# An MLP up-projection in seven block products for eight, on three token blocks for two

## The chip, the cores and the metric

One NeuronCore of one Trainium2 chip runs the whole program in one launch. The metric is the device time of one execution in microseconds (us), the median of several runs. The core has five engines with a queue each: TensorE (PE; its weight loads are shown apart as PEld), VectorE (DVE), ScalarE (ACT), GpSimd (POOL) and SyncE (SP), which here only starts DMAs. An engine works its queue in order.

## The reference, cut to what matters

One step of a one-layer streaming encoder: 2048 prompt tokens and 32 sample tokens, model width 1024. A norm, one input projection, four head groups (pooling, band attention, gated DeltaNet, GLA), and an output projection added to x give the residual x. The change touches only what follows, on 2080 tokens:

```python
h2 = _rmsnorm(x, mlp_norm_g[l])
up = jnp.square(jax.nn.relu(jnp.einsum('btd,df->btf', h2, w_up[l])))      # 1024 -> 4096
x = x + jnp.einsum('btf,fd->btd', up, w_down[l])                           # 4096 -> 1024
y = _rmsnorm(x, final_norm_g)
```

All tensors are float32. The matmuls take the type fp32r, whose values are shorter than float32; so each operand is split into a high part (a cast on ScalarE) and a low part (source minus high part, on VectorE), and each product is three matmuls: high x high, high x low, low x high.

## The kernel before

Everything is kept transposed: features lie on the 128 partitions, tokens along a row. Phase 1 (head groups and output projection) ends by storing the residual to a DRAM tensor `x2d`, feature tile by feature tile. Phase 2 is the MLP, and the change lies there.

Tokens are done in two blocks (`span`): 1024 tokens in two chunks of 512, then 1056 in three of 352. For each block, `mlp_acc` loads the residual into eight SBUF tiles `acc` (1024 features = 8 x 128), `mlp_norm` sums the squares and gets the reciprocal root into `nss` (in the profile; `self.ss` in the code), and `mlp_prep` writes the normed, scaled rows as high and low parts into `h2T`, a tile of one buffer. For block 0 this runs beside the end of the output projection: the generators are stepped between its matmuls. For block 1 the steps are taken between the output tiles of `mlp_down`, the norm from feature pair 13 on and the preparation in pair 15's turn.

The 4096 hidden features are 32 tiles of 128, taken in 16 pairs `f2`. `mlp_up(f, ...)` loads the 128 columns of w_up (1024 x 128, as a 128 x 1024 tile `wur`), splits them into two weight tiles, and for each chunk runs 8 k-tiles x 3 matmuls into one PSUM bank `u` (three buffers). Then Relu on ScalarE, max(u, 0) x relu(u) on VectorE (L1654), and the split into the tile `u`. `mlp_down` (L1658 to L1691) takes the pair before: for each chunk and each of the 8 output tiles it runs 2 x 3 matmuls into a bank `d` (three buffers), and VectorE adds the bank to `acc` (L1672). In the last pair of a block the squares of the finished `acc` are summed there (L1682 to L1687), and `final` (L1693) norms the chunk and stores it.

The order of the work: the program order above is a list of priorities. A planner in the compiler runs through it with estimated times and fixes each engine's queue, so matmuls of `mlp_up` and `mlp_down` come mixed in TensorE's queue; matmuls into one bank keep their order (`PT.order`, L96). Tiles come from pools with a fixed number of buffers taken in turn: `ld` (4) for everything loaded, `wt` (6) and `wx` (3) for weight parts, two from `wt` for one from `wx`. `wx` and the tiles `u` lie where phase 1's `hT` was and are to be had when the output projection is through. All helper matmuls are recorded under L90, all splits under L252 and L253 (L255 and L256 with a scale). Loads are started by SP, stores by ScalarE's queue.

Of the kernel before, what the change touches and what calls it, by code (L numbers as in the profile page):

```python
# [110 lines left out]
class K:  # L111
# [1417 lines left out]
    def span(self, blk):  # L1529

        return (SEQ // 2, SEQ // 2 + NS, 352, (2, 3, 4)) if blk else (0, SEQ // 2, 512, (0, 1))

    def mlp_acc(self, blk, acc):
        t0, n, _, gs = self.span(blk)
        for i in range(8):
            x = self.ac.tile([P, 1056], F32, name="acc", tag=f"acc{i}")[:, 0:n]
# [14 lines left out]
    def mlp_rows(self, blk, acc, i):  # L1551
# [3 lines left out]
        x = x[:, 0:n]  # L1555
        if acc is None:
            assert self.ready(*(("x2", g) for g in gs))
            self.nc.sync.dma_start(x, self.x2d[i][:, t0:t0 + n])
        return x, (x if acc is None else acc[i])

    def mlp_norm(self, blk, acc=None):

        nc = self.nc
        t0, n, cw, _ = self.span(blk)
        self.ss = ss = self.nm.tile([P, 1056], F32, name="nss", tag="nss")[:, 0:n]
        for i in range(8):
            x, src = self.mlp_rows(blk, acc, i)
            nc.scalar.activation(x if i else ss, src, AF.Square)  # L1568
# [3 lines left out]
        for o in range(0, n, cw):  # L1572
            self.rstd([ss[:, o:o + cw]], cw)
        yield

    def mlp_prep(self, blk, hT, acc=None):

        nc = self.nc
        n = self.span(blk)[1]
        nxt = self.mlp_rows(blk, acc, 0)  # L1580
        for i in range(8):
            x, src = nxt
            (nc.gpsimd if i % 2 or blk else nc.vector).tensor_tensor(x, src, self.ss, ALU.mult)
            self.split(hT[:, i, 0, 0:n], hT[:, i, 1, 0:n], x, self.mg[:, i:i + 1])
            if i < 7:
                nxt = self.mlp_rows(blk, acc, i + 1)
            yield

    def phase2(self):
        nc, tc, a = self.nc, self.tc, self.a  # L1590
        with ExitStack() as ctx:
# [3 lines left out]
            def wtile():  # L1595
                nwt[0] += 1
                if nwt[0] % 3:
# [3 lines left out]
            def weights(src, shape):  # L1601
                raw = self.ld.tile([P, 4 * 280], F32, name="wur", tag="ld")[:, 0:D]
                hi, lo = wtile(), wtile()
                view = (lambda x: x.rearrange("p (k f) -> p k f", k=8)) if shape else (lambda x: x)
                nc.sync.dma_start(view(raw), src)
                self.split(hi, lo, raw)
                return view(hi), view(lo)
# [5 lines left out]
            hT = self.h2.tile([P, 8, 2, 1056], F32R, name="h2T", tag="h2T")  # L1613
            with tc.tile_pool(name="wk2", bufs=1, **early) as self.wk:
# [10 lines left out]
                for z, _ in enumerate(self.fill):  # L1625
                    if self.last_part and not first:
                        first.append(weights(a["w_up"][0], True))
# [8 lines left out]
            rl = pool("rl2", 2)  # L1636
            self.wx = pool("wx", 3)
# [174 lines left out]
```

## Time and profile before

| | |
|---|---|
| median of 3 runs | 2767.6 us (2766.8 to 2770.08) |
| the profiled execution | 2760.96 us, span 2759.2 us |
| mean granted TensorE clock | 0.986 of full |
| TensorE / weight loads busy | 97% / 85% of the span |
| VectorE / ScalarE / GpSimd busy | 60% / 34% / 22% |
| first matmul of the MLP | at 1272 us of the span |
| moved by DMA | 292.88 MB, 106 GB/s in the mean |

One execution is recorded. Busy times are sums of recorded instructions; matmuls are pipelined, so one matmul's own duration (0.32 us at 352 columns) is longer than the distance to the next. The rate is read as a stretch of time over the number of matmuls in it.

### The profile page before, as it was taken

The page shows a single profiled execution, that of the slowest core. Times are in us where ns is not written, and L with a number is a line of the kernel's source. Part 1 is how long each engine was busy: PE and PEld are TensorE (multiplying, and loading weights), DVE is VectorE, ACT ScalarE, POOL GpSimd, SP SyncE. Part 2 cuts the span into 40 slices and gives each one's busy share as a digit, 9 for nine tenths or more (in the row PEclk, how much of TensorE's full clock was granted, in tenths as well). Part 3 has the DMA queues.
Part 4 walks back from the last instruction along what each step waited for, and adds up shares of the span by engine and source line. Part 5 has one row for each costly group of instructions (what it writes and reads, how often), then busy time and mean ns, then how long its engine had stood idle before and what let it go on. Part 6 is the DMA issues. An engine that isn't in the chain of part 4 may idle for free.

```text
span 2759.2 us, 41285 instructions
## 1 busy us (share of the span) xinstructions
PE 2670.6 (97%) x16044; PEld 2344.7 (85%) x16044; DVE 1652.4 (60%) x3081; ACT 933.2 (34%) x1758; POOL 620.6 (22%) x869
## 2 busy tenths in 40 slices
PE   7998998999899999989999999999999999999998
PEld 7887887888778887868888888888799999999997
DVE  6577688868876965574444445454755454545444
ACT  6535534653564343343121212131322121212122
POOL 4533554455446343230000000010300000000001
PEclk9998999999999999999999999999999999999999
DMA  5654454454546475465111112141341111111101
GB/s 173 191 158 141 135 164 142 137 162 132 167 123 175 131 224 167 131 197 170 46 46 46 54 38 61 31 124 31 112 167 54 39 54 39 54 39 48 45 31 63
DMA packets 195267, 292.88 MB, mean 106 GB/s; under 512 B 41344, under 2 KB 129680, under 8 KB 195072
## 3 DMA queue, kind: packets, MB, share of 16 engines
q1 hardware_dynamic: 123344, 231.58, 27.5%
q10 hardware_dynamic: 71664, 58.59, 6.5%
q8 instruction: 126, 2.06, 0.3%
q14 instruction: 69, 0.57, 0.1%
q0 software_dynamic: 64, 0.08, 0.0%
HBM read 227.67 MB, written 63.64 MB: 106 GB/s over the span
## 4 chain that ended last, share of the span: by engine, by line
PE 82%; DVE 9%; DMA 4%; issue 2%; ACT 2%; POOL 1%; SPq 0%; ACTq 0%; DVEq 0%; POOLq 0%
PE d L90 28%; PE u L90 26%; PE g L90 17%; PE s L90 4%; PE a L90 3%; PE l L90 2%; DVE wt L253 1%; PE s L94 1%; DVE tp L999 1%; DMA x2d<-sg 1%; DVE X L1000 1%; DVE h2T L256 1%; PE a L94 1%; DMA ldt<-w_o 1%; DVE hT L256 0%
## 5 line engine op out<-in xcount | busy, mean ns | idle before, releaser
L1672 DVE TENSOR_TENSOR acc<-acc,d 128x352 f32<-128x352 f32 (+1 forms) x616 | 360.5, 588 | 500.5 <-PE d L90 495.7
L90 PE MATMUL u<-h2T,wt 128*128 128x352 f32 (+1 forms) x2536 | 634.5, 352 | 0.0
L90 PE MATMUL d<-u,wt 128*128 128x352 f32 (+1 forms) x2576 | 624.7, 352 | 3.9 <-DVE acc L1672 3.9
L90 PE MATMUL g<-hT,wt 128*128 128x512 f32 (+2 forms) x2544 | 539.9, 361 | 15.6 <-ACT hT L252 4.7
L90 PEld LDWEIGHTS d<-u,wt 128*128 128x128 f32 x2576 | 455.5, 188 | 52.3 <-DVE acc L1672 7.0
L90 PEld LDWEIGHTS u<-h2T,wt 128*128 128x128 f32 x2536 | 451.8, 188 | 45.3 <-issue 0.5
L90 PEld LDWEIGHTS g<-hT,wt 128*128 128x128 f32 x2544 | 411.5, 192 | 80.9 <-issue 6.3
L90 PE MATMUL u<-h2T,wx 128*128 128x352 f32 (+1 forms) x1304 | 390.2, 350 | 0.0
L90 PE MATMUL d<-u,wx 128*128 128x352 f32 (+1 forms) x1264 | 356.7, 351 | 0.3 <-DVE acc L1672 0.3
L1653 ACT ACTIVATE rr<-u 128x352 f32<-128x352 f32 (+1 forms) x160 | 81.0, 515 | 635.8 <-PE u L90 594.9
L90 PEld LDWEIGHTS u<-h2T,wx 128*128 128x128 f32 x1304 | 238.9, 188 | 22.4
L90 PEld LDWEIGHTS d<-u,wx 128*128 128x128 f32 x1264 | 228.5, 188 | 22.2 <-DVE acc L1672 0.8
L90 PE MATMUL g<-wt,hT 128*128 128x256 f32 (+3 forms) x1632 | 240.8, 297 | 3.7 <-DVE sg L464 2.7
L90 PEld LDWEIGHTS g<-wt,hT 128*128 128x128 f32 (+1 forms) x1632 | 212.9, 188 | 14.6 <-issue 4.4
L253 DVE TENSOR_TENSOR wt<-ldt,wt 128x1024 fp32r<-128x1024 f32 (+1 forms) x120 | 163.2, 1360 | 65.0 <-ACT wt L252 64.4
L1687 POOL TENSOR_TENSOR fs<-fs,sq 128x352 f32<-128x352 f32 (+1 forms) x15 | 17.0, 1132 | 767.4 <-ACT sq L1685 767.4
L252 ACT CAST wt<-ldt 128x1024 fp32r<-128x1024 f32 (+1 forms) x120 | 126.0, 1050 | 114.2 <-PE g L90 66.0
L1570 POOL TENSOR_TENSOR nss<-nss,xp 128x1024 f32<-128x1024 f32 (+1 forms) x8 | 19.5, 2438 | 627.3 <-ACT xp L1568 619.4
L252 ACT CAST wt<-wur 128x1024 fp32r<-128x1024 f32 x85 | 87.7, 1045 | 185.1 <-PE u L90 101.0
L1654 DVE SCALAR_TENSOR_TENSOR rr<-u,rr 128x352 f32<-128x352 f32 (+1 forms) x160 | 92.7, 587 | 79.0 <-ACT rr L1653 78.4
L252 ACT CAST u<-rr 128x352 fp32r<-128x352 f32 (+1 forms) x160 | 82.9, 539 | 115.9 <-PE d L90 59.4
L253 DVE TENSOR_TENSOR u<-rr,u 128x352 fp32r<-128x352 f32 (+1 forms) x160 | 95.4, 617 | 23.1 <-ACT u L252 19.6
(329 smaller groups left out, 3336.1 us busy)
## 6 DMA issues: line engine op xcount, KB each, us to landing
wur<-w_up SPq DMA_DIRECT2D x64, 512.0 KB, 3.5
wur<-w_down SPq DMA_DIRECT2D x64, 512.0 KB, 3.5
ldt<-w_fm SPq DMA_DIRECT2D x56, 512.0 KB, 4.4
ldt<-w_o SPq DMA_DIRECT2D x32, 512.0 KB, 5.1
ldt<-w_tm SPq DMA_DIRECT2D x24, 512.0 KB, 4.2
fmd<-sg ACTq DMA_DIRECT2D x46, 256.0 KB, 2.8
qkr<-fmd SPq DMA_DIRECT2D x88, 128.0 KB, 3.9
xp<-x2d SPq DMA_DIRECT2D x16, 528.0 KB, 4.0
```

Source lines behind the costliest of these rows:

```text
L90: return self.order(self.k.nc.tensor.matmul(out, lhsT, rhs, start=not have, stop=True, skip_group_check=True))
L94: return self.order(self.k.nc.tensor.transpose(out, src, self.k.c["ident"][:n, :n]))
L252: nc.scalar.copy(hi, src)
L253: (eng or nc.vector).tensor_tensor(lo, src, hi.bitcast(F32), ALU.subtract)
L256: nc.vector.scalar_tensor_tensor(lo, src, scale, hi.bitcast(F32), ALU.mult, ALU.subtract)
L999: v.tensor_tensor(tv, bc(B[:, w:32, q:w], [P, r, w]), bc(X[:, q:w, 0:w], [P, r, w]), ALU.mult)
L1000: v.tensor_tensor(X[:, w:32, 0:w], X[:, w:32, 0:w], tv, ALU.subtract)
L1570: (nc.gpsimd if i % 2 else nc.vector).tensor_tensor(ss, ss, x, ALU.add)
L1653: nc.scalar.activation(rr[:, :cw], ps.t[:, :cw], AF.Relu)
L1654: nc.vector.scalar_tensor_tensor(rr[:, :cw], ps.t[:, :cw], 0.0, rr[:, :cw], ALU.max, ALU.mult)
L1672: nc.vector.tensor_tensor(x, x, ps.t[:, :cw], ALU.add)
L1687: (nc.vector if i % 2 else nc.gpsimd).tensor_tensor(fs[i % 2], fs[i % 2], sq, ALU.add)
```

## The change

Three token blocks of 696, 696 and 688 tokens, each of two equal chunks of h = 348 or 344, replace the two. `mlp_up` takes a pair of feature tiles at once. With A the pair's weights in 2 x 2 blocks (feature tile x half of the 1024 inputs) and B the block's input in 2 x 2 blocks (half of the inputs x half of the tokens), it forms seven products of sums (Strassen's method in Winograd's form) where the plain way has eight. `mlp_prep` writes seven input combinations of h columns each, `h2T` being 4 x 2 x 7 x 348, and `up_weights` builds the weight sums on GpSimd. Products are added up in PSUM where they can be; three are copied out or summed on the way. The bank `u` becomes three banks of one buffer each, u1, u2 and u4, and u1 takes four products in turn. Square and Relu are laid out anew: Relu on ScalarE, the square on GpSimd, over 696 tokens at once.

Weight parts come in turn from `wt` and `wx`, which has 6 buffers now; a pair uses 11 (A 2, s2/s4 2, s1 1, s3/A22 2, w_down 4). In the last pair of every block `mlp_down` takes the last two pairs together (in the kernel before only in the last block).

```diff
     def span(self, blk):
-        return (SEQ // 2, SEQ // 2 + NS, 352, (2, 3, 4)) if blk else (0, SEQ // 2, 512, (0, 1))
+        return ((0, 696, 348, (0, 1)), (696, 696, 348, (1, 2)), (1392, 688, 344, (2, 3, 4)))[blk]
...
+    COMB = {n: z for z, n in enumerate(("B11", "T3", "T1", "B21", "B22", "T2", "T4"))}
     def mlp_prep(self, blk, hT, acc=None):
-            (nc.gpsimd if i % 2 or blk else nc.vector).tensor_tensor(x, src, self.ss, ALU.mult)
-            self.split(hT[:, i, 0, 0:n], hT[:, i, 1, 0:n], x, self.mg[:, i:i + 1])
+        for k in range(4):
+            xa, sa = self.mlp_rows(blk, acc, k)
+            xb, sb = self.mlp_rows(blk, acc, k + 4)
+            nc.vector.scalar_tensor_tensor(xa[:, 0:n], sa, self.mg[:, k:k + 1], self.ss, ALU.mult, ALU.mult)
+            nc.scalar.mul(xb[:, 0:n], sb, self.mg[:, k + 4:k + 5])
+            nc.gpsimd.tensor_tensor(xa[:, n:n + h], xa[:, 0:h], xa[:, h:n], ALU.subtract)
+            nc.gpsimd.tensor_tensor(xb[:, 0:n], xb[:, 0:n], self.ss, ALU.mult)
+            yield
+            nc.gpsimd.tensor_tensor(xa[:, h:n], xb[:, h:n], xa[:, h:n], ALU.subtract)
+            nc.vector.scalar_tensor_tensor(xb[:, n:n + h], xa[:, n:n + h], -1.0, xb[:, h:n], ALU.mult, ALU.subtract)
+            self.split(hT[:, k, 0, 0:3 * h], hT[:, k, 1, 0:3 * h], xa[:, 0:3 * h])
+            yield
+            nc.vector.scalar_tensor_tensor(xa[:, 0:h], xb[:, n:n + h], -1.0, xb[:, 0:h], ALU.mult, ALU.subtract)
+            self.split(hT[:, k, 0, 3 * h:6 * h], hT[:, k, 1, 3 * h:6 * h], xb[:, 0:3 * h])
+            yield
+            self.split(hT[:, k, 0, 6 * h:7 * h], hT[:, k, 1, 6 * h:7 * h], xa[:, 0:h])
             yield
...
-                if nwt[0] % 3:
+                if nwt[0] < 3 or nwt[0] % 2:
                     return self.wtile()[:, 0:D]
...
+            def up_begin(f2):
+                r0, r1 = (raw(a["w_up"][2 * f2 + z].rearrange("p k f -> p (k f)")) for z in range(2))
+                return r0, r1, pair(r0)
+
+            def up_weights(r0, r1, A):
+                H = 512
+                s1 = self.nm.tile([P, H], F32, name="s1", tag="s1")
+                add = lambda o, x, y: nc.gpsimd.tensor_tensor(o, x, y, ALU.add)
+                add(s1, r1[:, 0:H], r1[:, H:D])
+                add(r1[:, 0:H], r0[:, 0:H], r1[:, 0:H])
+                add(r0[:, 0:H], s1, r0[:, 0:H])
+                add(r0[:, H:D], r0[:, 0:H], r0[:, H:D])
+                s24 = pair(r0)
+                w1 = wtile()
+                self.split(w1[:, 0:H], w1[:, H:D], s1)
+                s3a = pair(r1)
...
-            pu = pool("pu", 3, space=PSUM)
+            pu = pool("pu", 1, space=PSUM)
...
+            def mlp_up(f2, hT, h):
+                w = up_weights(*(first.pop() if first else up_begin(f2)))
...
+                def mm(z, x, y):
+                    hi, lo = w[x]
+                    o = self.COMB[y] * h
+                    for k in range(4):
...
+                        ps[z].mm(ps[z].t[:, :h], 0, P, hi[:, ks], bh)
+                        ps[z].mm(ps[z].t[:, :h], 0, P, hi[:, ks], bl)
+                        ps[z].mm(ps[z].t[:, :h], 0, P, lo[:, ks], bh)
+                def save(z, n):
+                    keep[n] = rl.tile([P, 348], F32, name="k", tag=f"k{n}")[:, :h]
+                    nc.scalar.copy(keep[n], ps[z].t[:, :h])
+                def total(z, n, o):
+                    nc.vector.tensor_tensor(o, keep[n], ps[z].t[:, :h], ALU.add)
+                def square(z):
+                    nc.gpsimd.tensor_tensor(c[z], c[z], c[z], ALU.mult)
+                    self.split(us[z][:, 0], us[z][:, 1], c[z])
+
+                mm(1, "A11", "B11")
+                save(1, 1)
+                mm(2, "A12", "B21")
+                total(2, 1, c[0][:, 0:h])
+                mm(1, "s2", "T2")
+                save(1, 2)
+                mm(4, "s1", "T1")
+                save(4, 5)
+                mm(1, "s3", "T3")
+                total(1, 5, c[1][:, h:n])
+                nc.scalar.activation(c[1][:, h:n], c[1][:, h:n], AF.Relu, scale=-1.0)
+                mm(4, "s4", "B22")
+                total(4, 2, c[0][:, h:n])
+                nc.scalar.activation(c[0], c[0], AF.Relu)
+                square(0)
+                self.tick()
+                mm(1, "A22", "T4")
+                nc.scalar.activation(c[1][:, 0:h], ps[1].t[:, :h], AF.Relu, scale=-1.0)
+                square(1)
...
-                    if blk and f2 == 15:
-                        mlp_down(us + nxt, acc, chs, t0)
+                    if f2 == 15:
+                        mlp_down(us + nxt, acc, chs, blk, side)
```

## Rows read from the trace of the kernel before

**Rows 1.** The page's first part, whole span: busy us, share, instructions of each engine.

```profile
span 2759.2 us, 41285 instructions
...
PE 2670.6 (97%) x16044; PEld 2344.7 (85%) x16044; DVE 1652.4 (60%) x3081; ACT 933.2 (34%) x1758; POOL 620.6 (22%) x869
```

**Rows 2.** The page's fourth part: shares of the chain of work by engine.

```profile
PE 82%; DVE 9%; DMA 4%; issue 2%; ACT 2%; POOL 1%; SPq 0%; ACTq 0%; DVEq 0%; POOLq 0%
```

**Rows 3.** Busy time by stretch: length, engines with instruction counts, PEclk, DMA share, GB/s.

```profile
1200.00:1272.00 72.00, 64.30 (x423) 59.70 (x422) 48.14 (x47) 27.89 (x27) 10.27 (x4) 0.93 0.65 208
...
1500.00:1700.00 200.00, 200.00 (x867) 162.37 (x866) 91.17 (x125) 34.83 (x49) 0.00 (x0) 1.00 0.15 45
1940.00:1968.00 28.00, 24.07 (x98) 17.41 (x97) 25.57 (x25) 12.35 (x13) 13.19 (x5) 1.00 0.45 144
2100.00:2300.00 200.00, 200.00 (x1241) 200.00 (x1240) 95.68 (x171) 37.59 (x66) 0.00 (x0) 1.00 0.14 43
2300.00:2600.00 300.00, 300.00 (x1863) 300.00 (x1863) 147.04 (x261) 61.07 (x106) 0.00 (x0) 1.00 0.16 48
```

**Rows 4.** Waits of TensorE's MLP, 1240 to 2759: total us, times, longest us.

```profile
PE d L90 <- DVE acc L1672: 4.1, 7, 1.5
```

**Rows 5.** Timeline, TensorE, 1249 to 1276: start, us, line, names, shapes, count.

```profile
1249.43 22.81 PE L90 MATMUL g<-hT,wt 128*128 128x288 f32 x168 [0.18 <-DVE sg L1402]
1272.08 1.08 PE L90 MATMUL u<-h2T,wt 128*128 128x512 f32 x4
```

**Rows 6.** Groups by form, 1350 to 2759: count, busy us, mean ns, idle before.

```profile
L1672 DVE TENSOR_TENSOR acc<-acc,d 128x352 f32<-128x352 f32 x360 | 185.9, 520 | 234.6 <-PE d L90 230.0 <-DMA acc<-x2d 4.2
...
L253 DVE TENSOR_TENSOR wt<-wur,wt 128x1024 fp32r<-128x1024 f32 x40 | 48.9, 1223 | 44.8 <-PE u L90 34.0 <-ACT wt L252 10.8
...
L252 ACT CAST wx<-wur 128x1024 fp32r<-128x1024 f32 x40 | 41.9, 1046 | 112.6 <-PE u L90 110.1 <-DMA wur<-w_up 2.5
...
L1653 ACT ACTIVATE rr<-u 128x352 f32<-128x352 f32 x96 | 42.8, 461 | 302.4 <-PE u L90 301.1 <-DVE u L253 0.9
...
L1583 POOL TENSOR_TENSOR xp<-xp,nss 128x1056 f32<-128x1056 f32 x8 | 22.6, 2831 | 103.3 <-DMA xp<-x2d 103.1
...
L1687 POOL TENSOR_TENSOR fs<-fs,sq 128x512 f32<-128x512 f32 x6 | 8.3, 1376 | 42.9 <-ACT sq L1685 42.9
```

**Rows 7.** Timeline of VectorE in block 1, 2309 to 2312.

```profile
2309.30 1.23 DVE L253 TENSOR_TENSOR wt<-wur,wt 128x1024 fp32r<-128x1024 f32 x1 [1.85 <-ACT wt L252]
2310.44 0.95 DVE L1672 TENSOR_TENSOR acc<-acc,d 128x352 f32<-128x352 f32 x2
```

**Rows 8.** Timeline of VectorE at the change of block.

```profile
1944.81 1.31 DVE L256 SCALAR_TENSOR_TENSOR h2T<-xp,pv,h2T 128x1056 fp32r<-128x1056 f32 x1
...
1958.44 2.32 DVE L256 SCALAR_TENSOR_TENSOR h2T<-xp,pv,h2T 128x1056 fp32r<-128x1056 f32 x1
1960.68 1.27 DVE L1672 TENSOR_TENSOR acc<-acc,d 128x512 f32<-128x512 f32 x2
1961.88 2.33 DVE L256 SCALAR_TENSOR_TENSOR h2T<-xp,pv,h2T 128x1056 fp32r<-128x1056 f32 x1
1964.12 1.21 DVE L253 TENSOR_TENSOR wx<-wur,wt 128x1024 fp32r<-128x1024 f32 x1
```

**Rows 9.** Timeline of GpSimd at the change of block.

```profile
1896.60 2.48 POOL L1583 TENSOR_TENSOR xp<-xp,nss 128x1056 f32<-128x1056 f32 x1 [59.37 <-DMA xp<-x2d]
...
1950.30 12.78 POOL L1583 TENSOR_TENSOR xp<-xp,nss 128x1056 f32<-128x1056 f32 x4 [9.77 <-DMA xp<-x2d]
```

**Rows 10.** Timeline of TensorE at the change of block, with what it waited for.

```profile
1961.41 0.95 PE L90 MATMUL d<-u,wt 128*128 128x512 f32 x3 [0.39 <-DVE acc L1672]
...
1965.99 0.96 PE L90 MATMUL d<-u,wt 128*128 128x512 f32 x3 [1.52 <-DVE acc L1672]
```

**Rows 11.** Timeline of VectorE, first addition of block 1.

```profile
2033.36 0.52 DVE L1672 TENSOR_TENSOR acc<-acc,d 128x352 f32<-128x352 f32 x1 [4.23 <-DMA acc<-x2d]
```

**Rows 12.** The page's sixth part: DMA issues, KB each, us to landing.

```profile
wur<-w_up SPq DMA_DIRECT2D x64, 512.0 KB, 3.5
```

More of the change, by code (lines that the diff above doesn't have):

```diff
@@ L1626, in phase2 @@
                     if self.last_part and not first:
-                        first.append(weights(a["w_up"][0], True))
+                        first.append(up_begin(0))
                     next(prep, None)
@@ L1635, in phase2 @@
             up = pool("up", 4)
[L1636 to L1638 removed]
+            rl = pool("rl2", 1)
+            self.wx = pool("wx", 6)
+            pu = pool("pu", 1, space=PSUM)
             pdn = pool("pdn", 3, space=PSUM)
[L1641 to L1642 removed]
+            def mlp_up(f2, hT, h):
+                w = up_weights(*(first.pop() if first else up_begin(f2)))
@@ L1656, in mlp_up @@
-                return u
-            def mlp_down(us, acc, chs, t0, side=None):
-                ws = [weights(a["w_down"][128 * f:128 * f + 128], False) for f, _ in us]
+                n = 2 * h
+                us = [up.tile([P, 2 * 696], F32R, name="u", tag="u")[:, 0:2 * n].rearrange("p (z n) -> p z n", z=2) for _ in range(2)]
+                ps = {z: PT(self, pu, [P, 512], f"u{z}") for z in (1, 2, 4)}
+                c = [rl.tile([P, 696], F32, name="c", tag=f"c{z}")[:, 0:n] for z in range(2)]
@@ L1661, in mlp_down @@
+                square(0)
[3 more added lines that the diff above has]
+                square(1)
+                return [(2 * f2, us[0]), (2 * f2 + 1, us[1])]
+            def mlp_down(us, acc, chs, blk, side=None):
+                ws = [pair(raw(a["w_down"][128 * f:128 * f + 128])) for f, _ in us]
                 done = us[-1][0] == 31
@@ L1690, in mlp_down @@
                     if done:
-                        self.spawn(final(acc, ts, t0, fs, t0 and ts is chs[-1]))
+                        self.spawn(final(acc, ts, self.span(blk)[0], fs, blk == 2 and ts is chs[-1]))
             def final(acc, ts, t0, fs, end):
@@ L1721, in phase2 @@
                         acc = []
-                        for _ in self.mlp_acc(1, acc):
+                        for _ in self.mlp_acc(blk, acc):
                             pass
-                    if blk and f2 == 15:
-                        mlp_down(us + nxt, acc, chs, t0)
-                    elif us is not None:
-                        mlp_down(us, acc, chs, t0, side)
+                    if f2 == 15:
+                        mlp_down(us + nxt, acc, chs, blk, side)
+                    elif us:
+                        mlp_down(us, acc, chs, blk, side)
                     us = nxt
```

85 lines of the change are left out of this document (37 added, 48 removed).

## The prediction

> **What bounds the kernel now.** The busy shares come first: TensorE is busy 97% of the span, VectorE 60% [rows 1], and the chain of work that ended last is TensorE for 82% of its length [rows 2]. Shares are averages, so the stretches come next. In the MLP TensorE has no idle time at all at full granted clock, both in the first token block (1500 to 1700) and in the second (2100 to 2600), while VectorE is at 46 to 49% there [rows 3]. The list of waits confirms it: over the whole MLP TensorE waited 4.1 us for VectorE, in 7 waits, and all of that is in the change of block, 1940 to 1968, where VectorE is at 91% and TensorE lost 28.0 - 24.1 = 3.9 us [rows 3, 4]. So the MLP ends when TensorE has streamed its columns; any column taken away is time, until VectorE or ScalarE fails to empty a PSUM bank in time.
>
> **Part 1: TensorE's columns.** Before, w_up and w_down each take 16 pairs x 96 matmuls of 512 columns in block 0 and 16 x 144 of 352 in block 1: together 3072 and 4608. One costs 200 us/867 = 0.2307 us at 512 and 300 us/1863 = 0.1610 us at 352 [rows 3]: 708.7 + 741.9 = 1450.6 us. After, a pair of feature tiles takes 7 products x 4 k-tiles x 3 = 84 matmuls up and 96 down (8 output tiles x 2 chunks x 6): 180 x 16 x 2 = 5760 of 348 columns and 2880 of 344. No row has those widths. The nearest are 352 and 288: 168 matmuls of 288 ran from 1249.43 to 1272.08, 0.1348 us each [rows 5]; that is 0.41 ns a column between them, so 0.1594 us at 348 and 0.1577 us at 344. Sum 918.1 + 454.2 = 1372.3 us: **78 us less**. Bounds: if a matmul can't go below what 352 costs, 8640 x 0.1610 = 1391 us, 60 us less; at the rate per column of the 512 form, 0.451 ns, 1349 us, 101 us less. I take 78, the value next to the 352 row.
>
> **Part 2: the work that the other engines get.** A pair now lasts 180 x 0.1594 = 28.7 us of TensorE. From 0.520 us at 352 and 1.223 us at 1024 elements [rows 6] a VectorE operation costs 0.15 us + 1.05 ns an element: 0.69 at 512, 0.88 at 696. Per pair VectorE has 5 whole low parts of weights (A, s2/s4, s3/A22, two of w_down; 6.1 us), the low part of s1 (0.69), three sums from PSUM (1.6), two low parts of u (1.8) and 16 additions to acc (8.3): 18.4 us, 64% of the pair, where before it was 49%. ScalarE has 5 casts at 1.045, the half cast, three copies out of PSUM at 0.46, three Relus and two casts of u [rows 6]: about 10.4 us, 36%. GpSimd, idle in these stretches before [rows 3], gets four additions of 512 at 1.376 us and two squares of 696, between that and 2.83 us for 1056, say 1.8 us [rows 6]: 9 us, 31%. By average all of this lies beside TensorE, and costs nothing where the order lets it.
>
> **Part 3: what is late when.** Two kinds of waits are new. Inside the seven products one bank is added to again while its earlier content must first be copied out (ScalarE) or summed (VectorE); one product of 12 matmuls, 1.91 us, is the cover. Copying takes 0.46 us and a cast of 1.045 us may stand ahead of it: 1.5 us, covered. A sum on VectorE takes 0.52 us with up to one low part ahead, 1.74 us: just covered, and late if that low part is held up. If it is late, everything on TensorE queues behind the waiting matmul, the w_down groups too.
>
> Second, the w_down groups, one each 6 x 0.1594 = 0.96 us over three banks, leave VectorE 1.9 us from the end of a group until its bank is wanted. One weight low part ahead of two additions, 1.23 + 0.95 us, cost TensorE nothing [rows 4, 7]. But VectorE is not alone any more. While GpSimd ran its multiplications from 1950.30, VectorE's h2T operations took 2.32 us instead of 1.31, and GpSimd's own took 12.78/4 = 3.2 us instead of 2.48; additions from PSUM kept their 0.63 us each, two in 1.27 [rows 8, 9]. One such long operation was followed by a TensorE wait of 0.39 us, two weight or h2T operations in a row (2.33 + 1.21) by one of 1.52 us [rows 8, 10]. The page "SBUF — State Buffer" of the Trainium skill (section "SBUF: two separate sides") has the rule behind this: VectorE with two SBUF inputs and GpSimd hold one port pair in turn, each for a whole instruction. The trace agrees for its h2T and acc operations; by that rule the weight and u low parts of Part 2 (8.6 us a pair) would meet all the new GpSimd work and the sums from PSUM would not, which speaks against the change and is priced as the third case below.
>
> I count per pair some two to three of the 7 two-input operations meeting GpSimd (busy 31%), half of them second, each 1.0 us longer (2.32 - 1.31); in a stretch of w_down groups 1.22 + 1.0 + 0.52 us exceeds the 1.9 us by 0.8, elsewhere nothing is lost. That is about 0.5 us a pair, x 48 = **24 us**. The bounds are far apart: 0 (block 1 of before had no wait of TensorE beyond those of the list [rows 4]), and 14% of the pair, 4.0 us, if every pair went as 1940 to 1968 did: 193 us. At an estimated 18.4 + 2.5 = 21 us, 73%, the pair lies between the 49% and the 91% stretch; I take the value near the former, since TensorE lost only 14% with VectorE almost full.
>
> **Part 4: changes of block, start and end.** There are now two changes of block. Preparing a block costs VectorE per k-pair 0.88 + 2 x 0.52 + 2 x 1.24 + 0.52 = 4.9 us, 19.7 us in all (8 x 1.31 = 10.5 before), GpSimd about 4 x 3.6 = 14 us, both on SBUF. h2T has one buffer, so nothing of it is written before the last product of the old block; TensorE's cover is the w_down of the last two pairs, 192 x 0.1594 = 30.6 us. In it VectorE has the preparation, 16 additions (8.3), some squares' sums (3) and weight low parts (4), 35 us, plus holds of about 1 us on 8 operations. The first product needs nine tenths of the preparation: 40 - 31 = 9 us lost a change, 18 us for two, less the 3.9 us of before: **+14 us** (0 to 36). Reloading acc is hidden: its first addition came at 2033.36 after a wait for the DMA without any wait of TensorE [rows 4, 11]; the cover shrinks to two w_up pairs, 2 x 84 x 0.1594 = 27 us.
> At the start the first preparation lies in the output projection, where VectorE was busy 48 of 72 us and TensorE already lost 8 [rows 3]; the longer preparation and the first weight sums, for which only 24 matmuls (3.8 us) give cover, cost **+4 us** (0 to 10). The extra norm of the third block is 1 us of matmuls. Weights are read three times, not twice: 2.1 MB a pair, 73 GB/s, while 208 GB/s were moved in 1200 to 1272 [rows 3]; a load lands in 3.5 us [rows 12] and its buffer is free most of a pair ahead, so it is counted at nothing; SP issues 64 more of them, with only other loads (weights, acc, xp) queued behind. The end (two chunks, not three, in the last block) is the same chain: nothing.
>
> **Sum.** -78 + 24 + 14 + 4 + 1 = -35 us. The profiled execution's own time is 2760.96 us (span 2759.2 and 1.8 around it); less 35 that is 2726. The median of the runs is 2767.6, 6.6 us above the profiled one, so **2732.6 us** is predicted.
>
> **The rivals.**
> - All of the gain stays: waits of TensorE are near nothing, as in 2100 to 2600 with 48% VectorE, since the order was planned ahead and banks leave slack; the changes of block cost as before. Then -78 + 4 + 1 to 10 more: about 2700 us. For it: VectorE had idle time in each d group [rows 7]. Against it: VectorE at two thirds and GpSimd beside it.
> - The matmuls don't get cheaper with 4 columns less, since weight loading is what paces them: its unit is busy 100% in the 352 stretches and 81% in the 512 ones [rows 3]. Then Part 1 gives 60, not 78: 2751 us. Against it: 288 columns ran at 0.1348 us [rows 5].
> - VectorE becomes the bound (the other side). GpSimd's 9 us, if all of it holds VectorE up, make its 18.4 us a pair 27.4 of 28.7, 95%, as in 1940 to 1968. At the 4.0 us a pair lost there: 2767.6 - 78 + 19 + 193 = 2902 us; at half of it, as holds fall on either engine, 2805 us, the time I give it. It decides against the change from (78 - 19)/48 = 1.2 us a pair on. For it: the long operations and waits of [rows 8, 10]. Against it: 8.3 + 1.6 us of VectorE's work reads PSUM and isn't held.
>
> **Chances.** The forecast 0.55, from 0.2 to 0.9 us a pair and 5 to 25 us at the changes of block: 2708 to 2758. The full gain 0.19, weight loading 0.06, VectorE as the bound 0.20. About 0.2% (5.5 us) is what a measurement of this kernel tells from no change. Faster: 0.53 + 0.19 + 0.05 = 0.77; the same: 0.02 + 0.01 + 0.04 = 0.07; slower 0.16 of the last. The range goes from 2697 (the lower end of the full gain) to 2790 (short of the middle of the VectorE case), leaving out about 0.04 below and 0.12 above.
>
> **What would show it.** Part 1: 348-column matmuls 0.159 us apart in unbroken stretches. Part 2: VectorE at 65 to 75% and GpSimd at 30% in the MLP. Part 3: TensorE waits on acc additions or on the copies and sums of the up products, 24 us in all; weight low parts of 2 us and more where GpSimd is busy. Part 4: two gaps of some 9 us around the changes of block, ended by h2T. It is wrong if TensorE's waits exceed 60 us, if an up product waits for weights pair after pair, or if a matmul of 348 columns takes 0.165 us or more.

## The result, and the profile after

The changed kernel takes 2728.4 us (median of 4 runs, 2727.5 to 2732.8), the kernel before 2767.2 in the same comparison: ratio 0.9866, 95% interval [0.9846, 0.9886]. Predicted were 2732.6. The profiled execution after took 2728.74 us, 32.2 less than that of before; the sum of the prediction was 35 less.

The page of after, its first and fourth part, beside [rows 1, 2]:

```profile
span 2727.0 us, 44461 instructions
...
PE 2604.8 (96%) x17012; PEld 2407.6 (88%) x17012; DVE 1881.1 (69%) x3330; ACT 1144.1 (42%) x2034; POOL 1067.2 (39%) x1188
...
PE 75%; DVE 12%; DMA 4%; ACT 3%; issue 3%; POOL 3%; SPq 0%; ACTq 0%; DVEq 0%; POOLq 0%
```

TensorE lost 65.8 us of busy time, but the span only 32.2: its share fell from 97 to 96%, and 7% of the chain went over to other engines. The stretches of after, columns as in [rows 3]:

```profile
1200.00:1272.00 72.00, 55.94 (x361) 52.07 (x361) 49.96 (x54) 28.59 (x31) 17.67 (x11) 0.88 0.57 186
...
1700.00:1800.00 100.00, 84.73 (x484) 80.12 (x483) 82.88 (x99) 46.94 (x72) 53.71 (x35) 0.93 0.44 138
...
1725.00:1735.00 10.00, 7.23 (x24) 6.78 (x25) 9.32 (x12) 5.86 (x10) 5.57 (x4) 0.50 0.29 73
...
1800.00:2000.00 200.00, 200.00 (x1260) 200.00 (x1259) 126.19 (x189) 70.47 (x101) 59.79 (x43) 1.00 0.25 74
...
2170.00:2300.00 130.00, 114.56 (x659) 110.32 (x658) 98.88 (x125) 56.87 (x86) 60.93 (x40) 0.93 0.39 123
...
2210.00:2220.00 10.00, 7.25 (x22) 6.36 (x23) 8.34 (x12) 4.67 (x9) 2.15 (x2) 0.50 0.42 109
...
2400.00:2600.00 200.00, 200.00 (x1272) 200.00 (x1271) 130.06 (x192) 70.49 (x101) 61.52 (x43) 1.00 0.25 74
```

Three things are to be seen. Inside a block TensorE is as full as before: 200.00 of 200 us at full clock, with VectorE at 63 to 65% and GpSimd at 30 to 31%. Around the two changes of block it is idle for 15.3 us (1700 to 1800) and 15.4 us (2170 to 2300); the one change of before lost 3.9 us [rows 3]. And in the output projection it lost 16.1 of 72 us, where it lost 7.7 before. The waits of TensorE's MLP of after, as in [rows 4]:

```profile
PE d L90 <- ACT u L252: 12.3, 5, 4.7
PE d L90 <- DVE u L253: 8.7, 7, 4.6
PE d L90 <- DVE acc L1749: 5.6, 4, 2.8
```

Before there was one kind of wait, for acc, 4.1 us. Now most of the time goes to u: the down matmuls wait for the activations of their own pair. The timeline of TensorE at the first change shows where (columns as in [rows 5]):

```profile
1720.83 0.75 PE L90 MATMUL d<-u,wt 128*128 128x348 f32 x3 [4.06 <-ACT u L252]
1726.17 0.66 PE L90 MATMUL d<-u,wt 128*128 128x348 f32 x1 [4.60 <-DVE u L253]
```

After 1726.17 TensorE runs on at a granted clock of 0.50, the 1.2 GHz level, for some 10 us (the stretch 1725 to 1735 above: 24 matmuls in 7.23 us, which at 0.159 us each are 3.8). It had been idle for most of the ten microseconds ahead. At the second change the same: 22 matmuls in 7.25 us. These two stretches cost 3.4 + 3.8 = 7 us beside the idle time.

VectorE of after in the same microseconds:

```profile
1719.17 4.57 DVE L253 TENSOR_TENSOR h2T<-xp,h2T 128x1044 fp32r<-128x1044 f32 x2 [2.54 <-ACT h2T L252]
...
1725.25 0.87 DVE L253 TENSOR_TENSOR u<-c,u 128x696 fp32r<-128x696 f32 x1
```

and GpSimd of after:

```profile
1715.86 1.98 POOL L1711 TENSOR_TENSOR c<-c 128x696 f32<-128x696 f32 x1
1717.80 0.92 POOL L1594 TENSOR_TENSOR xp<-xp 128x348 f32<-128x348 f32 x1
...
1720.29 2.35 POOL L1711 TENSOR_TENSOR c<-c 128x696 f32<-128x696 f32 x1
```

The squares of the last pair (L1711) stand on GpSimd among the operations that prepare the next block (L1594, and L1595, left out here), and their low parts (u<-c,u) on VectorE behind h2T low parts that take 4.57/2 = 2.3 us each. Read in order of time, this is one chain: GpSimd square, ScalarE cast, VectorE low part, TensorE.

Groups of VectorE by form after, 1310 to 2690, beside [rows 6]:

```profile
L1749 DVE TENSOR_TENSOR acc<-acc,d 128x348 f32<-128x348 f32 x478 | 240.6, 513 | 215.7 <-PE d L90 215.2
...
L253 DVE TENSOR_TENSOR wt<-wur,wx 128x1024 fp32r<-128x1024 f32 x111 | 142.7, 1287 | 30.6 <-ACT wx L252 15.8 <-PE u L90 12.2 <-issue 0.7
...
L253 DVE TENSOR_TENSOR u<-c,u 128x696 fp32r<-128x696 f32 x62 | 68.7, 1118 | 6.8 <-ACT u L252 6.8
```

Operations from SBUF alone are longer beside GpSimd (weights 1.287 us for 1.223; u 1.118, where the forecast worked out 0.88), those that read PSUM are not (0.513 at 348 columns, for 0.520 at 352).

**The balance by milestones.** The first up product of after:

```profile
1278.62 0.79 PE L90 MATMUL u<-h2T,wt 128*128 128x348 f32 x4
```

It starts at 1278.6 after, at 1272.08 before [rows 5]: 6.5 us lost ahead of it. From there to the end of the span, 2727.0 - 1278.6 = 1448.4 for 2759.2 - 1272.1 = 1487.1: 38.7 us gained. The columns give 83.8 of these (below), so 45 us of the gain are given back inside the MLP. The changes of block account for 15.3 + 15.4 + 7 - 3.9 = 34 of them. Some 7 more lie in the same two stretches, in TensorE's busy time: it was busy 199.3 us there, for 472 + 647 matmuls of the MLP, which are some 177 us at the distance they have inside a block, and 8 us of the norm's matmuls; of the 14 us left, the two ten-microsecond stretches above hold 7. The rest is small idle times.

### The profile page after: what moved, and what is told of

Same layout as the page of the kernel before. It is cut to its first block, busy times and chain, and to the rows that moved or that the text cites. A ratio compares the mean times of both kernels' runs of the same rounds, so it can differ in the third digit from the quotient of the medians.

```text
span 2727.0 us, 44461 instructions
## 1 busy us (share of the span) xinstructions
PE 2604.8 (96%) x17012; PEld 2407.6 (88%) x17012; DVE 1881.1 (69%) x3330; ACT 1144.1 (42%) x2034; POOL 1067.2 (39%) x1188
## 4 chain that ended last, share of the span: by engine, by line
PE 75%; DVE 12%; DMA 4%; ACT 3%; issue 3%; POOL 3%; SPq 0%; ACTq 0%; DVEq 0%; POOLq 0%
PE d L90 26%; PE u L90 20%; PE g L90 18%; PE s L90 4%; PE a L90 3%; PE l L90 2%; DVE h2T L253 1%; DVE wt L253 1%; PE s L94 1%; DVE acc L1778 1%; DVE tp L999 1%; DVE X L1000 1%; POOL wur L1638 1%; PE a L94 1%; DMA xp<-x2d 1%
## 5 line engine op out<-in xcount | busy, mean ns | idle before, releaser
L90 PE MATMUL d<-u,wt 128*128 128x348 f32 (+1 forms) x2400 | 638.6, 325 | 26.7 <-ACT u L252 12.3
L90 PE MATMUL d<-u,wx 128*128 128x348 f32 (+1 forms) x2208 | 600.0, 322 | 0.0
L1749 DVE TENSOR_TENSOR acc<-acc,d 128x348 f32<-128x348 f32 (+1 forms) x720 | 361.9, 511 | 344.7 <-PE d L90 344.0
L90 PE MATMUL g<-hT,wt 128*128 128x512 f32 (+2 forms) x2544 | 541.3, 362 | 23.5 <-ACT wt L252 12.5
L90 PE MATMUL u<-h2T,wx 128*128 128x348 f32 (+1 forms) x2008 | 515.2, 322 | 7.4 <-ACT k L1705 4.3
L90 PE MATMUL u<-h2T,wt 128*128 128x348 f32 (+1 forms) x2024 | 516.6, 321 | 0.1
L90 PEld LDWEIGHTS d<-u,wx 128*128 128x128 f32 x2208 | 398.1, 189 | 0.3
L90 PEld LDWEIGHTS u<-h2T,wx 128*128 128x128 f32 x2008 | 354.0, 188 | 10.0 <-ACT k L1705 5.1
L1711 POOL TENSOR_TENSOR c<-c 128x696 f32<-128x696 f32 (+1 forms) x96 | 151.4, 1578 | 147.6 <-ACT c L1731 96.9
L253 DVE TENSOR_TENSOR wx<-wur,wt 128x1024 fp32r<-128x1024 f32 x125 | 160.5, 1287 | 24.0 <-ACT wt L252 14.8
L253 DVE TENSOR_TENSOR wt<-wur,wx 128x1024 fp32r<-128x1024 f32 x114 | 147.3, 1295 | 35.2 <-ACT wx L252 20.3
```

The lines of the kernel that those rows point to most:

```text
L90: return self.order(self.k.nc.tensor.matmul(out, lhsT, rhs, start=not have, stop=True, skip_group_check=True))
L253: (eng or nc.vector).tensor_tensor(lo, src, hi.bitcast(F32), ALU.subtract)
L1711: nc.gpsimd.tensor_tensor(c[z], c[z], c[z], ALU.mult)
L1749: nc.vector.tensor_tensor(x, x, ps.t[:, :cw], ALU.add)
```

## The experiments

Each was compared with the kernel before. The change alone is 0.9866 [0.9846, 0.9886], some 37 us; differences between two experiments below about 0.0025, 7 us, are not told apart, and a difference given below is uncertain by about as much.

**Three blocks without the seven products.** The kernel before with the new blocks alone:

```diff
-        return (SEQ // 2, SEQ // 2 + NS, 352, (2, 3, 4)) if blk else (0, SEQ // 2, 512, (0, 1))
+        return ((0, 696, 348, (0, 1)), (696, 696, 348, (1, 2)), (1392, 688, 344, (2, 3, 4)))[blk]
...
-            for blk in range(2):
+            for blk in range(3):
...
```

> The kernel before with the three token blocks of 696, 696 and 688 alone, every product and the preparation as before (eight products for eight, last two w_down pairs apart). Theory (the lost time lies in what Strassen's preparation does to the queues): 6144 matmuls of 348 at 0.1587 us and 3072 of 344 at 0.1572 us make 1458 us against 1450.6, one more change of block at the 3.9 us of before and 1 us for a norm: about 12 us more than before in the profiled execution, 2773 us, and TensorE's waits at each change near 4 us. Rival (a change of block costs 15 us with these blocks, whatever the products): two of them at 15 us of waits and 4 us of half clock, 2800 us.

Measured 2776.5 us, 1.0034 [1.0023, 1.0045]. Eight products in these blocks are 6144 matmuls of 348 columns and 3072 of 344, at the prices of after 975.1 + 482.9 = 1458.0 us for 1450.6: 7.4 of the some 9 us. A second change of block by itself thus costs nearly nothing, and its largest kind of wait in the MLP stays what it was [rows 4]:

```profile
PE d L90 <- DVE acc L1672: 3.5, 5, 1.1
```

So the 15 us per change belong to the work that the seven products bring, not to the blocks.

**The order of the queues at a change.** First theory: u is late only because it stands behind the preparation in in-order queues; put it ahead, and the idle time goes. Three kernels. In the first the down groups of the last two pairs are not merged:

```diff
-                for f2 in range(16):
-                    nxt = mlp_up(f2, hT, h)
+                for f2 in range(16 + (blk < 2)):
+                    nxt = mlp_up(f2, hT, h) if f2 < 16 else []
...
-                    if f2 == 15:
+                    if f2 == 15 and blk == 2:
```

> The changed kernel, but in the first two blocks w_down of the pairs 14 and 15 runs one after the other, as in the kernel before. Theory (TensorE runs dry after the last up product because the parts of u of pair 15 stand in the queues behind the preparation, and every w_down group needs them): pair 14 alone gives 96 matmuls, 15.3 us, that need none of it; the waits of 4.1 and 4.6 us and some 4 us of matmuls at the lower clock go at each change, 16 more additions of 0.51 us come: 2703 to 2715 us. Rival (VectorE's sum of work in the preparation is what sets the change): the same wait turns up later, ahead of the first product of the next block, 8 us longer by the additions: 2728 to 2745 us.

Measured 2731.1, 0.9877 [0.986, 0.9894]: no gain. TensorE's waits from 1650 to 2400:

```profile
PE d L90 <- ACT wt L252: 20.3, 2, 10.7
PE d L90 <- DVE acc L1749: 11.3, 13, 2.0
```

and the queue of SP from 1690 (start and duration in us, DMA and count):

```profile
1695.84 31.93 SPq L1557 DMA_DIRECT2D xp<-x2d  x6
1738.51 3.08 SPq L1621 DMA_DIRECT2D wur<-w_down  x2
```

and what SP waited for in 1690 to 1760:

```profile
SPq L1621 <- DVE xp L1601: 12.9, 2, 10.6
```

The wait for u is gone, but the last pair's weights are now issued behind the loads of xp, and then wait 10.6 us more, until 1738.5, for a buffer in which VectorE still works on an xp. In the second kernel the preparation is ordered behind the last pair's square, cast and low part on each of the three engines (`g` adds that order to each operation, by its queue's letter; `sp` does the same around `split`):

```diff
+                    q = nc.gpsimd.tensor_tensor(c[z], c[z], c[z], ALU.mult)
+                    self.ahead = (q, *self.split(us[z][:, 0], us[z][:, 1], c[z]))
...
+            g("v", nc.vector.scalar_tensor_tensor(xa[:, 0:n], sa, self.mg[:, k:k + 1], self.ss, ALU.mult, ALU.mult))
...
+            sp(hT[:, k, 0, 0:3 * h], hT[:, k, 1, 0:3 * h], xa[:, 0:3 * h])
...
```

> The changed kernel, but every operation of the preparation of the blocks 1 and 2 is ordered behind the square and the split of pair 15 in its engine's queue. Theory (order in the queues): from the last product Relu 0.45, square 1.65, cast 0.77 and low part 0.88 us are 3.8 us, about what the 24 w_down matmuls that need only pair 14 cover; the waits of 4.1 and 4.6 us shrink to 0 to 2 us and the clock does not fall; the preparation starts some 5 us later, of which half comes back ahead of h2T: 2710 to 2722 us. Rival (sum of work): what is won there is lost ahead of the next block's first product, 2726 to 2735 us.

Measured 2741.0, 0.9913 [0.9896, 0.9929]: slower than the change. Its waits in the same stretch:

```profile
PE u L90 <- ACT wt L252: 24.2, 5, 11.1
```

and SP's queue:

```profile
1696.23 43.24 SPq L1558 DMA_DIRECT2D xp<-x2d  x8
1758.77 3.57 SPq L1636 DMA_DIRECT2D wur<-w_up  x3
```

u is nearly on time (waits of 1.4 us for its casts and 1.0 us for its low parts), but xp's buffers come free later, so SP stands longer at xp, and the next block's first weights are issued at 1758.8, where after they are at 1741.2. In both runs the theory was out. The rival's time fits the first run, though the wait came for weights of w_down and not ahead of the next block's first product; the second was slower than either range. The third is the first with the weights of both pairs issued ahead of the preparation (`down_weights` is the loading and splitting of w_down, taken out of `mlp_down`):

```diff
+                    if f2 == 15 and blk < 2:
+                        ws = down_weights(us + nxt)
+                        mlp_down(us, acc, chs, blk, side, ws[:2])
+                        mlp_down(nxt, acc, chs, blk, side, ws[2:])
...
```

> Pairs 14 and 15 of w_down one after the other in the first two blocks, as in the run before with that edit, but the weights of both are loaded and split ahead of the preparation. Theory (there the 9.6 and 10.7 us waits were weights of pair 15 whose loads stood behind the preparation's rows in the load buffers; without that the order is good): these waits go, with them the lower clock, no wait for parts of u: 2702 to 2714 us. Rival (VectorE, busy 9.3 to 10 of 10 us from 1720 to 1750, sets the change whatever the order): a wait of some 10 us comes back ahead of the first product of the next block: 2725 to 2735 us.

Measured 2725.5, 0.9868 [0.9852, 0.9885]. Its waits from 1650 to 2400, ahead of its stretch at the first change:

```profile
PE d L90 <- DVE acc L1752: 19.5, 16, 3.5
```

and the stretch:

```profile
1680.00:1800.00 120.00, 104.81 (x618) 100.31 (x617) 97.57 (x129) 55.93 (x84) 59.14 (x39) 0.97 0.33 99
```

Neither u (0.8 us) nor weights (2.5 us) are late by much, and the loss at the first change is the same 15 us, at the second 13: now the additions to acc are late, sixteen times. The queue theory falls; the rival's time came true, but again not the place of its wait. It looks as if the order only decides which of VectorE's operations is the late one, and what it has to do, at the lengths that it has there, doesn't fit under TensorE's work. That is argued here; the runs on GpSimd below test it. The same with five load buffers:

```diff
-        self.ld = pool("ld", 4)
+        self.ld = pool("ld", 5)
```

> The same with five load buffers. Theory of the load buffers: 4 to 8 us better than with four, at the start (the wait of 12.5 us became 9.7 with five) and at the first weights of each block: 2696 to 2710 us. Rival (VectorE's sum of work): 2722 to 2730 us.

Measured 2726.7, 0.9868 [0.9852, 0.9883], with 16.4 us of waits for acc: nothing more, as the rival had it.

**The start.** TensorE's longest wait in the output projection of after ends when weights of w_o have come and are cast:

```profile
1241.85 8.35 PE L90 MATMUL g<-hT,wt 128*128 128x256 f32 x45 [12.48 <-ACT wt L252]
```

SP's queue shows that they were issued late:

```profile
1235.43 4.07 SPq L276 DMA_DIRECT2D ldt<-w_o  x2
```

The preparation takes xp in pairs out of the four `ld` buffers that the weights of the output projection come through too, and holds each pair while seven forms of it are made. The fifth buffer alone:

> The changed kernel with five buffers for loads instead of four. Theory (the 12.5 us wait of TensorE in the output projection at the start comes from loads of w_o that wait for a buffer, since the preparation now holds two at a time): the wait shrinks to under 5 us, the first up product comes at about 1272 us instead of 1278.6: 2720 to 2724 us. Rival (VectorE and GpSimd are busy with the longer preparation, and the casts are late for that): no change, 2728 us.

Measured 2722.4, 0.9844 [0.9829, 0.9859], an interval that overlaps that of the change. The time lies in the theory's range, but not for its reason: the first up product starts only 1 us earlier (1277.5), and most of the wait is still there:

```profile
PE g L90 <- ACT wt L252: 9.7, 1, 9.7
```

Two buffers for xp alone, in all blocks:

```diff
-        x = self.ld.tile([P, 4 * 280], F32, name="xp", tag="ld")
+        x = self.xq.tile([P, 3 * 348], F32, name="xp", tag="xq")
...
+            self.xq = pool("xq", 2, **early)
```

> The changed kernel, but the rows that norm and preparation load or work in (xp) come from two buffers of their own, so the four load buffers are left to weights and mixer rows. Theory (load buffers held by the preparation make the loads of w_o and w_up late): the 12.5 us wait at the start falls below 3 us and the first up product comes at 1266 to 1272 us; at the changes of block no wait for a cast of w_up; 2715 to 2723 us. Rival (the load buffers are not what is short; with two buffers a k-pair's rows can't be fetched while the pair before is in work, 3.7 us of landing each): the start stays near 1277 us and each change gets 5 to 10 us longer, 2735 to 2745 us.

Measured 2729.4, 0.9871 [0.9853, 0.9889], between the two ranges. The start's wait is gone, but at the changes of block there are new ones (1680 to 2400):

```profile
PE u L90 <- ACT h2T L252: 12.3, 5, 8.6
PE g L90 <- POOL fs L1765: 9.4, 1, 9.4
```

SP's waits from 1680 to 1790 begin with

```profile
SPq L1557 <- DVE xp L1601: 40.4, 3, 15.9
```

where after has 18.6 us of this kind: the rows of the next k-pair can't be loaded while VectorE works on the pair before, as the rival had it, and the last long casts of h2T start at 1760.6, where after they start by 1745.5. So the theory was right for the start, and the rival for the changes of block, where two buffers are too few. With them in block 0 alone:

```diff
-        x = self.ld.tile([P, 4 * 280], F32, name="xp", tag="ld")
+        x = self.ld.tile([P, 4 * 280], F32, name="xp", tag="ld") if blk else self.xq.tile([P, 3 * 348], F32, name="xp", tag="xq")
...
-            with tc.tile_pool(name="wk2", bufs=1, **early) as self.wk:
+            with tc.tile_pool(name="wk2", bufs=1, **early) as self.wk, tc.tile_pool(name="xq", bufs=2, **early) as self.xq:
```

> The changed kernel, but in the first block alone, where xp is only scratch, norm and preparation work in two buffers of their own; the other blocks keep the load buffers. Theory (load buffers held by the first preparation make the loads of w_o late at the start; the changes of block are another matter): the 12.5 us wait goes as it did with own buffers in all blocks, from the norm's matmuls to the first up product it takes about 70 us instead of 84, and the changes of block stay as they are: 2714 to 2720 us. Rival (what is won at the start is lost to another wait of the output projection): 2726 to 2730 us.

Measured 2715.3, 0.9821 [0.9804, 0.9837]: about 12 us less than the change. The output projection's largest group of waits, 1200 to 1300, was 12.5 us for one weight and is now

```profile
PE g L90 <- DVE sg L1402: 3.7, 4, 1.5
```

and the first up product starts at 1267.5, not 1278.6.

**GpSimd beside VectorE.** What makes VectorE's operations too long for the change of block? Theory: GpSimd, by holding VectorE's operations up as in [rows 8], and through its own slow operations in u's and the weights' chains. Rival: VectorE simply has too many, so giving it GpSimd's costs more. The weight sums on VectorE:

```diff
-                add = lambda o, x, y: nc.gpsimd.tensor_tensor(o, x, y, ALU.add)
+                add = lambda o, x, y: nc.vector.tensor_tensor(o, x, y, ALU.add)
```

> The changed kernel with the four weight sums of a pair on VectorE instead of GpSimd: VectorE gets 4 x 0.69 = 2.8 us more a pair, 21 to 22 of 28.6 us, GpSimd keeps its squares. Theory (in the steady part the planned order leaves TensorE no wait as long as VectorE is well under its pair, here 75%): the stretches 1320 to 1650 and 1800 to 2000 stay at 100% TensorE, weight low parts fall from 1.287 to about 1.23 us: 2726 to 2732 us. Rival (the forecast's: VectorE near three quarters costs about half a us a pair): some 24 us more, 2750 us.

Measured 2716.0, 0.9829 [0.9814, 0.9843]: about 10 us faster than the change by the ratios, though VectorE has 4 x 48 = 192 operations more:

```profile
1320.00:1650.00 330.00, 330.00 (x2078) 330.00 (x2077) 235.12 (x355) 116.57 (x166) 41.21 (x25) 1.00 0.25 76
...
1700.00:1800.00 100.00, 87.61 (x501) 83.77 (x500) 85.47 (x113) 48.28 (x74) 34.23 (x23) 0.93 0.41 131
...
2170.00:2300.00 130.00, 120.08 (x721) 116.67 (x720) 108.43 (x148) 58.90 (x90) 40.54 (x26) 0.96 0.43 131
```

Inside the block VectorE's 71% still cost TensorE nothing, and the two changes lose 12.4 + 9.9 us for 15.3 + 15.4. The rival's slower time is out, and the theory's range began 10 us above the measured time. One thing went against the theory: the weights' low parts (1310 to 2690) did not get shorter,

```profile
L253 DVE TENSOR_TENSOR wt<-wur,wx 128x1024 fp32r<-128x1024 f32 x111 | 146.7, 1323 | 17.0 <-ACT wx L252 8.7 <-PE u L90 6.6
```

1.323 us for 1.287, though GpSimd is busy 41 of 330 us inside the block where it was 102; u's fell from 1.118 to 0.953. So the gain of this run is not that of shorter weight operations. From the other side, GpSimd's work raised (each square also written to an unused tile, the first weight sum formed three times):

```diff
-                add(s1, r1[:, 0:H], r1[:, H:D])
+                for _ in range(3):
+                    add(s1, r1[:, 0:H], r1[:, H:D])
...
+                spare = self.nm.tile([P, 696], F32, name="spare", tag="spare")
...
+                    nc.gpsimd.tensor_tensor(spare[:, 0:n], c[z], c[z], ALU.mult)
                     nc.gpsimd.tensor_tensor(c[z], c[z], c[z], ALU.mult)
```

> The changed kernel with GpSimd's work of every pair nearly doubled, with no use of the added results: each square is also written to a spare tile, and the first weight sum is formed three times: 2 x 1.58 + 2 x 1.40 = 6 us more, GpSimd at 51 to 55% of a pair. Theory (TensorE keeps its pace as long as VectorE with its holds stays under some 80% of the pair): the low parts get longer by 0.1 to 0.3 us each and the steady stretches stay at 99 to 100% TensorE; only the changes of block and the first pairs lose: 2728 to 2738 us. Rival (the forecast's price of half a us a pair and its third case, VectorE held up by GpSimd, which had only missed their size by a little): 24 to 60 us more, 2752 to 2790 us.

Measured 2749.0, 0.9947 [0.9929, 0.9965], 22 us more than the change and between the two expectations:

```profile
1320.00:1650.00 330.00, 329.38 (x2070) 329.10 (x2069) 232.70 (x314) 119.10 (x167) 186.05 (x115) 1.00 0.26 79
...
1700.00:1800.00 100.00, 80.67 (x451) 76.08 (x450) 80.75 (x92) 43.58 (x68) 57.44 (x38) 0.91 0.38 117
1800.00:2000.00 200.00, 199.88 (x1253) 199.01 (x1252) 142.90 (x191) 68.72 (x97) 113.76 (x74) 1.00 0.27 83
...
2170.00:2300.00 130.00, 111.67 (x648) 105.43 (x647) 102.21 (x121) 54.85 (x83) 74.36 (x51) 0.95 0.39 122
```

With GpSimd at 56 to 57% the inside of a block loses 0.7 us in 530. There VectorE was busy 142.90 us of 200 with 191 operations, for 126.19 with 189: that is holding, and it stays hidden. In the two stretches with a change of block TensorE issued 33 + 11 matmuls fewer than after; these 44 are 7 us at 0.159. Counted the same way, 26 fewer ran in 1250 to 1320, among the first pairs, and 19 fewer in 2000 to 2170, together another 7 us; the rest is spread, and none of it was traced to one wait. The preparation's GpSimd operations on VectorE instead, in blocks 1 and 2:

```diff
-            nc.gpsimd.tensor_tensor(xb[:, 0:n], xb[:, 0:n], self.ss, ALU.mult)
+            (nc.vector if blk else nc.gpsimd).tensor_tensor(xb[:, 0:n], xb[:, 0:n], self.ss, ALU.mult)
```

(and its two subtractions likewise)

> The changed kernel with the three GpSimd operations of a k-pair's preparation on VectorE in the blocks 1 and 2. Theory (the port that VectorE and GpSimd hold in turn sets the change of block: VectorE's preparation took 28 us there for 19.7 us of work, held up by GpSimd's): VectorE gets 4 x 1.92 = 7.7 us more work and loses about 8 us of holds, and no chain goes over GpSimd; TensorE's waits at each change fall from 15 to 8 to 12 us, 2716 to 2726 us. Rival (VectorE's own work sets it): 7.7 us more at each change, 2735 to 2744 us.

Measured 2725.6, 0.9858 [0.9839, 0.9877]: not told apart from the change. The rival's 2735 us and more is out. The waits moved little (1650 to 2400, where after has 11.3 and 7.9 us of these two):

```profile
PE d L90 <- ACT u L252: 10.7, 4, 3.8
PE d L90 <- DVE u L253: 5.4, 3, 3.1
```

**All of it together.** The start's two buffers, the weight sums and the preparation on VectorE, and the squares on ScalarE:

```diff
-                    nc.gpsimd.tensor_tensor(c[z], c[z], c[z], ALU.mult)
+                    nc.scalar.activation(c[z], c[z], AF.Square)
```

> The whole change with four edits: own token buffers in block 0 (as the start run), weight sums on VectorE, squares on ScalarE, and the preparation of blocks 1 and 2 without GpSimd. In the MLP GpSimd then runs only the small feature sums and the output's work beside VectorE. Theory (the rest of the loss is what GpSimd costs, by its own slow operations in the chains and by lengthened VectorE operations, and the start is a separate loss of the load buffers): the 13 us of the start run and the 12 us of the run with the sums on VectorE add up, and the squares and preparation without GpSimd give 3 to 10 more, 2698 to 2708 us. Rival (at a change of block the sum of VectorE's own operations sets the time, so moving more of them there gives nothing or costs): the start's 13 us remains and the sums' 12 us only in part, 2710 to 2718 us.

Measured 2686.1 us, 0.9714 [0.9698, 0.9729], below the whole range that the theory gave. Its stretches:

```profile
1700.00:1800.00 100.00, 93.89 (x556) 90.38 (x556) 86.58 (x134) 53.46 (x83) 8.05 (x6) 0.97 0.45 146
1800.00:2000.00 200.00, 200.00 (x1259) 200.00 (x1259) 137.46 (x216) 80.62 (x115) 0.00 (x0) 1.00 0.24 74
...
2170.00:2300.00 130.00, 124.52 (x752) 121.00 (x752) 106.37 (x166) 67.35 (x103) 7.17 (x6) 0.96 0.40 130
```

and three of its groups of VectorE, 1310 to 2640, as above for after:

```profile
L1749 DVE TENSOR_TENSOR acc<-acc,d 128x348 f32<-128x348 f32 x468 | 236.1, 513 | 162.6 <-PE d L90 159.2 <-DMA acc<-x2d 1.0 <-DMA o_y<-acc 0.4
...
L253 DVE TENSOR_TENSOR wt<-wur,wx 128x1024 fp32r<-128x1024 f32 x110 | 134.3, 1222 | 20.2 <-PE u L90 10.7 <-ACT wx L252 7.3 <-issue 0.4
...
L253 DVE TENSOR_TENSOR u<-c,u 128x696 fp32r<-128x696 f32 x60 | 52.5, 876 | 1.0 <-ACT u L252 1.0
```

VectorE runs 35 operations more than after in 1700 to 1800, in nearly the same time (86.58 us for 82.88), and TensorE issues 556 matmuls there for 484. The changes lose 6.1 + 5.5 us. In the two stretches TensorE issues 72 + 93 = 165 matmuls more than after, some 26 us. The whole gain over after, by the profiled spans, is 2727.0 - 2683.1 = 43.9 us, of which 14.6 lie ahead of the first up product, which starts at 1264.0; so nearly all that was won behind it was won at the changes. The low parts of the weights are back at the 1.22 us of before [rows 6], and u's at 0.876, the 0.88 of the forecast. The rule of the Trainium skill, page "SBUF — State Buffer", section "SBUF: two separate sides", is that VectorE with two SBUF inputs and a GpSimd operation that reads SBUF have one port pair in turn, for a whole instruction. The trace agrees: with GpSimd idle inside a block these two groups fall from 1.287 and 1.118 us, and the additions from PSUM stay at 0.513. How busy GpSimd is does not give the length by itself: with the sums alone moved, the weights' low parts took 1.323 us.

Against the change that is 0.9866 - 0.9714 = 0.0152, 42 us. By their own ratios the start's buffers give 12 of them and the weight sums 10; the other 20, if the parts add up, came with the squares on ScalarE and the preparation, of which the preparation alone gave 2, within its uncertainty. Whether the squares alone give the rest, or it takes a GpSimd free of all three, was not run. Nor do the runs part the held-up VectorE operations from GpSimd's slowness: a square took 1.6 us there and 0.78 on ScalarE, and stands in u's chain.

## Why the prediction came out

The total was right to 3 us in the profiled executions, and that is partly luck: two terms were wrong in opposite directions.

- **Columns, -78 us.** Right. 200 us hold 1260 matmuls of 348 columns and 1272 of 344: 0.1587 and 0.1572 us (forecast 0.1594 and 0.1577). 5760 x 0.1587 + 2880 x 0.1572 = 1366.8 us, 83.8 less than before. The rival that weight loading keeps a matmul at the 352 price, 0.161, is out.
- **The other engines' loads.** VectorE 64% and GpSimd 31% were forecast; 63 to 65% and 30 to 31% are there.
- **Holds inside a block, +24 us.** This step failed: TensorE waited for nothing there, 200.00 of 200 us, and for next to nothing with GpSimd at 56%. The size was wrong first. The forecast gave two to three operations a pair a full extra 1.0 us, the hold of [rows 8], where both engines ran back to back. Measured, the two low parts of u are 0.24 us longer each (1.118 for the 0.876 of the last run) and the five weight low parts 0.06, about 1 us a pair with s1's, not 2.5. Then the slack: with these holds spread out, no bank came late. The rival "all of the gain stays" was right about this stretch, and only here.
- **Changes of block, +14 us.** The step that was mis-sized the other way: 34 us measured, some 41 with the busy time of the balance above; the stated bounds were 0 to 36. Of its three causes the first was seen and underrated (VectorE full beside GpSimd: 82.88 of 100 us busy), and two were not in the sum: the squares of the last pair standing on GpSimd amid the preparation, so that the down groups came late at the beginning of the cover and not h2T at its end as forecast; and the half clock after the gaps, 7 us. The forecast counted VectorE's work against the cover, 40 for 31 us; it did not follow u's chain through three in-order queues. The queue experiments show that mending this chain by order only moves the loss, the last run that taking GpSimd out of it removes most of the loss.
- **Start, +4 us.** 6.5 measured, but not for the reason given. The forecast looked at VectorE and the cover of the first weight sums; the loss was a wait of 12.48 us for weights of w_o whose buffers xp held (before, TensorE waited 1.2 us for casts of such weights in 1200 to 1272). The two buffers of the start run took it away. The `ld` pool is shared by the rows (L1553) and the weights, and now each of two tiles lives through a longer preparation; that could have been read from the code.
- **VectorE as the bound.** Inside a block it did not come near: at 70 to 73% busy, with GpSimd at 11% or 57%, TensorE lost nothing or next to nothing.

So 24 us that did not come inside the blocks, and 6 more from the columns, stood in for some 27 at the changes beyond the 14, 2.5 at the start and a few of small losses elsewhere in the MLP, and the sum held.

## What to carry to other kernels

When work moves onto engines that idle, price it in the stretch where those engines are already full: here the steady stretch hid all of it, and the two short changes of block paid. Where a chain crosses three in-order queues, follow the last item of the old stage through each queue past everything that the new stage puts there, and look who shares a buffer pool with what now lives longer. When reordering only moves the wait from one tile to another with the same sum, stop reordering, and shorten the operations or take an engine out.

## What the runs showed that was not expected

- Giving VectorE 192 more operations, by taking them from GpSimd, made the kernel some 10 us faster; without GpSimd in the MLP's loops VectorE did 134 operations in 86.58 us, where it did 99 in 82.88.
- After two waits of 4.06 and 4.60 us, close together, TensorE's granted clock stood at 0.50 for about 10 us, and matmuls of 348 columns took 0.30 us (7.23/24). In the last run, with waits of 3.3 us at most, the clock of 1700 to 1800 was 0.97 for 0.93.
- Two buffers of its own for xp took the start's wait away in block 0 and brought new waits at the changes of block (9.4 us for fs, 12.3 us for h2T): there SP waited 40.4 us for VectorE to be through with an xp, for 18.6 after.
- With the weight sums moved to VectorE the weights' low parts took 1.323 us for 1.287, though GpSimd had less than half of its work left.
